# Rotary embedding of attention heads: gathering the rotated rows of all heads before turning them

## The chip, the cores and the metric

The kernel runs on one core of one Trainium2 chip. The metric is the device time of one execution in microseconds (us), and a kernel's time is the median of its runs. TensorE, the matrix engine, works beside VectorE, ScalarE and GpSimd; SyncE and ScalarE issue the transfers of this kernel. The engines run their own lists of instructions and wait for one another by semaphores. In the profile they are PE, DVE, ACT, POOL and SP.

## The reference

One layer over 512 tokens of width 1024, in fp32: a gated feed-forward network, a token mixer, and a second network, each followed by a layer norm of the input and the result. The mixer has two branches, sliding-window attention with sinks and a gated recurrence (HGRN2). Here only the attention's rotation matters: of each head's 64 values the first 16 are turned by an angle that depends on the token, in 16 heads of queries and 4 of keys.

```python
def partial_rope(t, cos, sin):
    half = ROPE_DIM // 2            # ROPE_DIM = 16, HEAD_DIM = 64
    t1, t2, rest = tf[..., :half], tf[..., half:ROPE_DIM], tf[..., ROPE_DIM:]
    return concatenate([t1 * cos - t2 * sin, t2 * cos + t1 * sin, rest], axis=-1)

q_a = partial_rope(q_a.reshape(B, S, N_Q_HEADS, HEAD_DIM), cos, sin)
k_a = partial_rope(k_a.reshape(B, S, N_KV_HEADS, HEAD_DIM), cos, sin)
y_attn = sliding_window_attention(q_a, k_a, v_a, sinks)
```

In the attention a block of 128 tokens sees its own block and the one before, and `exp(sink - m)` is added to the denominator of the softmax.

## The kernel before

**The products.** A matmul in fp32 is made of three in a rounded type: an operand is cut into a high part (`split`, a cast on ScalarE, L85) and a low part (the difference on VectorE, L86), called `whi` and `wlo` for weights. Each matrix of 1024 x 512 weights (a quad) goes through the class `Quads` in seven products of 24 matmuls of 128x256 each (`mul`, L276 to L293), in the order f1, then the previous quad's m4 and m3, f5, f6, f2, f7. Copies of sums in PSUM are kept by ScalarE (L313: `m1` after f1, `vs` after f6, `u3` after f7); VectorE adds them to others (L378, L323, L329) and makes the sums of weights (L308). A pipeline of depth 1 has the operands of the next product split while the present one runs. The pools are rings: four places for `whi` and `wlo`, five for raw weights, four PSUM banks named A for the products and four named B for all else.

**The side work.** Everything that is not such a product is put in between by the class `Side`: a list of generators, of which every half product takes as many steps as `side.rate` says; a step that yields `PAUSE` ends the turn. The rotation and the attention are such generators. The program runs `q_quad(0)`, then `gate_quad(0)` with `k_parts()` at its side (rate 1.0), then `gate_quad(1)`, `gate_quad(2)`, `q_quad(1)`, `gate_quad(3)` and a quad of the recurrence with `attention()` at their side (rate 3.0), L1021 to L1036. So the place of an instruction on its engine follows from these rates, and what the tile framework then makes of the order.

**The attention.** A tile holds two heads of 64 rows by 512 tokens. `k_parts` (L830) rotates the two key tiles and splits them for both partition halves. `q_quad(pp)` makes the queries of eight heads, four tiles; `q_parts(pp, ip)` (L857) adds the bias to each of two tiles (L865, ScalarE), rotates it and splits it into a high part (L871, ScalarE) and a low part (L872, VectorE). `chunk(pp, ip)` then goes over four blocks of tokens: `scores` (L889 and L890 on TensorE, the masking L894 on VectorE), `probs` (L901: exponentials on ScalarE by `func`, the sinks added in L912, sums and quotients in L916 to L920 on VectorE, transposes L124 on TensorE, copies L927 on ScalarE), and `weigh` (L942 on TensorE, copies L948 on ScalarE). `both` (L968) has the next `q_parts` run in between. For each of four chunks `q_parts` gives two tiles.

**The rotation.** `rope(dst)`, L797 to L802, works on a whole tile of 128 rows, though only 16 of each 64 are turned: the tables hold cos 1 and sin 0 for the other rows. It is four operations of VectorE on 128x512: a shuffle of rows within groups of 32 into `room(0)` (L799), times sin (L800), the tile times cos in place (L801), and the sum (L802). With two key tiles and eight query tiles that is ten sets.

Of the kernel before, what the change touches and what calls it, by code (L numbers as in the profile page):

```python
# [14 lines left out]
AF = mybir.ActivationFunctionType  # L15
ALU = mybir.AluOpType
# [6 lines left out]
S = 512  # L23
# [4 lines left out]
HD = 64  # L28
# [14 lines left out]
def body(ctx, tc, a):  # L43
    nc = tc.nc
# [31 lines left out]
    def big(i, shape=(P, 2, S), dtype=F32):  # L76

        return mid.tile(list(shape), dtype, name=f"g{i}")
# [42 lines left out]
    def transposed(blocks):  # L121
        tp = bank("B")
        for j, b in enumerate(blocks):
            nc.tensor.transpose(out=tp[:, j * P:(j + 1) * P], in_=b, identity=ident)  # L124
        return tp
# [74 lines left out]
    def func(**kw):  # L200


        with tc.issue_after(chain[-1]) if chain else ExitStack():
            chain.append(nc.scalar.activation(**kw).ins)
# [5 lines left out]
    PAUSE = object()  # L210
# [36 lines left out]
    side = Side()  # L247
# [19 lines left out]
    class Outs:  # L267
# [3 lines left out]
        def room(self, i):  # L271
            return self.rooms[i]
# [409 lines left out]
    def mix_const(name, shape, src=None, place=None):  # L682

        t = mc.tile(shape, F32, name=(place or name) + "_c")
        nc.sync.dma_start(out=t, in_=a[name] if src is None else src)
        return t
# [26 lines left out]
    cos_t = mix_const("rope_c", [P, S])  # L713
    sin_t = mix_const("rope_s", [P, S])
    amask = mix_const("amask", [P, 256])
    sink = mix_const("sinks", [P, NH], a["sinks"].broadcast_to([P, NH]))
# [22 lines left out]
    def bias(n, i):  # L739
        j = BCOL[n] + i  # L740
        return bcol[:, j:j + 1]
# [26 lines left out]
    def quad_to(src, d1, d2, done=None, mix=None):  # L768

        def finish(v):  # L770
            nc.scalar.copy(out=d2[:, :, :256], in_=v)
            if done:
                done()
        quads.quad(src, Outs((*thalves(d1), d2[:, :, 256:]), finish), mix)
# [17 lines left out]
    pairs = {0: Pair(0)}  # L792


    swap = [8 + i for i in range(8)] + list(range(8)) + list(range(16, 32))

    def rope(dst):  # L797
        rot = room(0)
        nc.vector.stream_shuffle(out=rot, in_=dst, mask=swap)  # L799
        nc.vector.tensor_tensor(out=rot, in0=rot, in1=sin_t, op=ALU.mult)  # L800
        nc.vector.tensor_tensor(out=dst, in0=dst, in1=cos_t, op=ALU.mult)  # L801
        nc.vector.tensor_tensor(out=dst, in0=dst, in1=rot, op=ALU.add)  # L802


    v_sb = big(5, [P, TT, 256])
# [18 lines left out]
    k_raw = [room(6 + j) for j in range(2)]  # L824
# [5 lines left out]
    def k_parts():  # L830


        k_hi.extend(big(i, dtype=F32R) for i in (4, 10))
        k_lo.extend(big(i, dtype=F32R) for i in (2, 11))
        for t in k_lo:
            nc.gpsimd.memset(t[top, 1].bitcast(F32), 0.0)
            nc.gpsimd.memset(t[bot, 0].bitcast(F32), 0.0)
        for j in range(2):
            t = k_raw[j]
            rope(t)  # L840
            yield
            for h, own in enumerate((top, bot)):
                for half in (top, bot):
                    nc.scalar.copy(out=k_hi[j][half, h], in_=t[own])
                nc.vector.tensor_tensor(out=k_lo[j][own, h], in0=t[own], in1=k_hi[j][own, h], op=ALU.subtract)
                yield

    q_raw = {}

    def q_quad(pp, mix=None):  # L850
# [3 lines left out]
            q_raw[pp] = d  # L854
        quad_to(a["w_q"][pp], d[0], d[1], done, mix)

    def q_parts(pp, ip):  # L857


        while pp not in q_raw:  # L860
            yield
        out = []
        for i in range(2):
            t = q_raw[pp][ip][:, i]
            nc.scalar.activation(out=t, in_=t, func=AF.Identity, bias=bias("q", 4 * pp + 2 * ip + i),  # L865
                                 scale=1.0 if ip == 0 else -1.0)
            rope(t)
            yield
            q = big(6 + 2 * ip + i, dtype=F32R)
            for h, (own, other) in enumerate(((top, bot), (bot, top))):  # L870
                nc.scalar.copy(out=q[own, h], in_=t[own])  # L871
                nc.vector.tensor_tensor(out=q[other, h], in0=t[own], in1=q[own, h], op=ALU.subtract)  # L872
                yield
            out.append(q)
        return out
# [25 lines left out]
    def probs(pp, n, ip, neg, nm):  # L901


        kb = 1 if n == 0 else 2
        sm = mxp.tile([P, 4], F32, name="sm", bufs=3)
        rd = mxp.tile([P, 4], F32, name="rd", bufs=3)
        for j in range(4):
            func(out=neg[j // 2][:, j % 2, :kb * P], in_=neg[j // 2][:, j % 2, :kb * P], func=AF.Exp,
                                 bias=nm[:, j:j + 1], scale=-1.0, accum_out=sm[:, j:j + 1])
        for hf in range(2):  # L910
            hh = 8 * pp + 4 * hf + 2 * ip
            nc.vector.tensor_tensor(out=rd[:, 2 * hf:2 * hf + 2], in0=nm[:, 2 * hf:2 * hf + 2],  # L912
                                    in1=sink[:, hh:hh + 2], op=ALU.add)
        yield
        func(out=rd, in_=rd, func=AF.Exp)
        nc.vector.tensor_tensor(out=rd, in0=rd, in1=sm, op=ALU.add)  # L916
        nc.vector.reciprocal(out=rd, in_=rd)
        for j in range(4):
            p_ = neg[j // 2][:, j % 2, :kb * P]
            nc.vector.tensor_scalar(out=p_, in0=p_, scalar1=rd[:, j:j + 1], scalar2=None, op0=ALU.mult)  # L920
        for _ in range(2):
            yield PAUSE
        tps = [transposed([neg[j // 2][:, j % 2, kk * P:(kk + 1) * P] for j in range(4)]) for kk in range(kb)]
        pts = []
        for kk in range(kb):
            pt = neg[kk].rearrange("p i c -> p (i c)") if n % 2 else room(6 + kk)
            nc.scalar.copy(out=pt, in_=tps[kk])  # L927
            pts.append(pt)
        return pts
# [21 lines left out]
    def chunk(pp, ip, qs):  # L951
        h = 4 * pp + 2 * ip
        pts = []
        ahead = yield from scores(pp, 0, ip, qs)
        for n in range(TT):
            now = ahead
            if n + 1 < TT:
                ahead = yield from scores(pp, n + 1, ip, qs)
            pts.append((yield from probs(pp, n, ip, *now)))
            yield PAUSE  # L960
            if n % 2:
                y = room(5, [P, 2, 2, P])
                weigh(pp, n - 1, pts[-2:], y)
                nc.sync.dma_start(out=ya_dram[h:h + 2, :, (n - 1) * P:(n + 1) * P].rearrange("i p c -> p i c"),
                                  in_=y.rearrange("p i n c -> p i (n c)"))
                yield
# [16 lines left out]
    def attention():  # L983
        qs = yield from q_parts(0, 0)
        for i in range(4):
            for _ in range(2):
                yield PAUSE
            if i < 3:
                nxt = yield from both(chunk(i // 2, i % 2, qs), q_parts((i + 1) // 2, (i + 1) % 2), 3)
                side.marks.append(i)  # L990
                qs = nxt
            else:
                yield from chunk(1, 1, qs)
# [24 lines left out]
    def gate_quad(i):  # L1018
        quads.quad(a["w_" + ("ga", "gh")[i // 2]][i % 2], Gates(i))

    q_quad(0, mix)  # L1021
    side.add(k_parts())
    side.rate = 1.0
    gate_quad(0)
    pipe.pump()
    side.add(attention())
    side.rate = 3.0
    gate_quad(1)
    gate_quad(2)
    while len(side.marks) < 1:  # L1030
# [287 lines left out]
def _rope_rows():  # L1318
    half = HD // 8
    inv = np.float32(500000.0) ** (-np.arange(0, 2 * half, 2, dtype=np.float32) / np.float32(2 * half))  # L1320
    ang = np.arange(S, dtype=np.float32)[:, None] * inv[None, :].astype(np.float32)
    cos, sin = np.cos(ang).T, np.sin(ang).T
    c = np.ones((HD, S), np.float32)
    s = np.zeros((HD, S), np.float32)
    c[:half], c[half:2 * half] = cos, cos
    s[:half], s[half:2 * half] = -sin, sin
    return np.concatenate([c, c]), np.concatenate([s, s])


# [59 lines left out]
```

## Time and profile before

| | |
|---|---|
| median of 3 runs | 1254.51 us (1254.0 to 1255.38) |
| profiled execution | 1255.64 us, its span 1253.8 us |
| granted clock of TensorE, mean | 0.997 |
| TensorE busy | 1228.7 us, 98% |
| VectorE busy | 992.0 us, 79% |
| ScalarE busy | 646.7 us, 52% |
| GpSimd busy | 37.1 us, 3% |

The span is what the profiler saw between the first and the last instruction; a run's time has some 2 us around it. The chain of work that ended last is followed back from the last instruction, at each step to what released it. A matmul's end is modelled, since matmuls are pipelined, so the distance between starts is the better measure of TensorE's pace. An idle time is shown with what ended it. In the windows, PEclk is the granted clock of TensorE as a share of its full 2.4 GHz.

### The profile page before, as it was taken

Reading aid. Unit: us, or ns where it says so; the run is one execution under the profiler, and the core shown is the slowest. Engines: PE = TensorE matmul, PEld = TensorE weight load, DVE = VectorE, ACT = ScalarE, POOL = GpSimd, SP = SyncE. Lnnn points to the kernel's source line nnn. Section 1 sums busy time; section 2 is a strip of 40 time slices with the busy share of each in tenths; the row PEclk is TensorE's granted clock in tenths of the full one; section 3 lists DMA queues with packets and bytes.
Section 4 is the critical chain, followed back from the end, with each engine's and each line's share of the span. In section 5 each row is a group of like instructions: output and inputs, shape, how many; then the busy total and the mean of one; then the engine's idle time right before and its main releaser. Section 6 shows DMA issues by size and latency. Waiting matters only on the chain.

```text
span 1253.8 us, 21589 instructions
## 1 busy us (share of the span) xinstructions
PE 1228.7 (98%) x8918; PEld 1155.2 (92%) x8918; DVE 992.0 (79%) x1389; ACT 646.7 (52%) x916; POOL 37.1 (3%) x37
## 2 busy tenths in 40 slices
PE   9999999999999999999999999999999999999997
PEld 9999999888899989989999998788899999998886
DVE  7988878983499999898878787564899887789535
ACT  5554455642247667677654765442364445466210
POOL 0000000000000000000001011000100000000001
PEclk9999999999999999999999999999999999999999
DMA  7433332742232344233223243653333333345301
GB/s 264 140 98 116 102 101 85 234 131 89 101 139 83 111 133 138 86 109 104 87 70 117 86 158 111 238 193 132 118 116 121 102 102 102 116 128 193 118 34 68
DMA packets 51715, 152.84 MB, mean 122 GB/s; under 512 B 5792, under 2 KB 12960, under 8 KB 51616
## 3 DMA queue, kind: packets, MB, share of 16 engines
q1 hardware_dynamic: 47296, 137.29, 32.9%
q10 hardware_dynamic: 4320, 14.16, 3.4%
q8 instruction: 70, 1.15, 0.4%
q14 instruction: 29, 0.24, 0.1%
HBM read 136.75 MB, written 14.68 MB: 121 GB/s over the span
## 4 chain that ended last, share of the span: by engine, by line
PE 80%; DVE 13%; DMA 2%; issue 2%; POOL 1%; ACT 1%; SPq 0%; DVEq 0%; ACTq 0%; POOLq 0%
PE A L293 47%; PE A L119 5%; PE A L118 5%; PE A L117 5%; PE A L618 4%; DVE wlo L86 3%; PE B L118 3%; PE B L117 3%; PE B L119 3%; DVE x L86 2%; PE B L124 2%; PE B L942 1%; POOL rstd L447 1%; DVE g L452 1%; PE B L618 1%
## 5 line engine op out<-in xcount | busy, mean ns | idle before, releaser
L293 PE MATMUL A<-x,whi 128*128 128x256 f32 x3840 | 544.1, 284 | 4.2 <-ACT u L313 3.1
L293 PEld LDWEIGHTS A<-x,whi 128*128 128x128 f32 x3840 | 496.1, 192 | 6.8 <-ACT u L313 4.1
L85 ACT CAST whi<-raw 128x1024 fp32r<-128x1024 f32 (+1 forms) x182 | 188.5, 1041 | 260.2 <-PE A L119 102.7
L293 PE MATMUL A<-x,wlo 128*128 128x256 f32 x1920 | 311.6, 284 | 0.2 <-DVE wlo L86 0.2
L86 DVE TENSOR_TENSOR wlo<-raw,whi 128x1024 fp32r<-128x1024 f32 (+1 forms) x182 | 219.3, 1208 | 114.1 <-ACT whi L85 113.7
L293 PEld LDWEIGHTS A<-x,wlo 128*128 128x128 f32 x1920 | 265.7, 192 | 0.9 <-issue 0.4
L85 ACT CAST whi<-wsum 128x1024 fp32r<-128x1024 f32 x140 | 146.5, 1049 | 154.1 <-PE A L293 118.3
L86 DVE TENSOR_TENSOR wlo<-wsum,whi 128x1024 fp32r<-128x1024 f32 x140 | 170.2, 1219 | 7.1 <-ACT whi L85 6.9
L117 PE MATMUL A<-whi,x 128*128 128x256 f32 (+1 forms) x280 | 87.7, 313 | 0.0
L118 PE MATMUL A<-wlo,x 128*128 128x256 f32 (+1 forms) x280 | 87.5, 313 | 0.0
L119 PE MATMUL A<-whi,x 128*128 128x256 f32 (+1 forms) x280 | 86.9, 311 | 0.0
L308 DVE TENSOR_TENSOR wsum<-raw 128x1024 f32<-128x1024 f32 x64 | 77.5, 1219 | 9.7 <-DMA raw<-in_w_dram 8.4
L308 DVE TENSOR_TENSOR wsum<-raw,wsum 128x1024 f32<-128x1024 f32 x64 | 78.1, 1220 | 0.6
L117 PE MATMUL A<-x,whi 128*128 128x512 f32 (+1 forms) x160 | 59.9, 374 | 0.1
L119 PE MATMUL A<-x,wlo 128*128 128x512 f32 (+1 forms) x160 | 59.3, 371 | 0.5 <-DVE wlo L86 0.5
L118 PE MATMUL A<-x,whi 128*128 128x512 f32 (+1 forms) x160 | 59.0, 369 | 0.0
L117 PEld LDWEIGHTS A<-whi,x 128*128 128x128 f32 x280 | 53.3, 190 | 3.0
L119 PEld LDWEIGHTS A<-whi,x 128*128 128x128 f32 x280 | 53.2, 190 | 2.9
L118 PEld LDWEIGHTS A<-wlo,x 128*128 128x128 f32 x280 | 53.3, 191 | 2.6
L86 DVE TENSOR_TENSOR x<-g,x 128x512 fp32r<-128x512 f32 (+1 forms) x57 | 47.9, 861 | 6.2 <-ACT x L85 6.1
L618 PE MATMUL A<-whi,x 128*128 128x512 f32 x192 | 51.1, 389 | 0.0
L85 ACT CAST x<-g 128x512 fp32r<-128x512 f32 (+1 forms) x57 | 42.2, 765 | 16.2 <-DVE g L1262 4.6
(202 smaller groups left out, 1632.6 us busy)
## 6 DMA issues: line engine op xcount, KB each, us to landing
raw<-in_w_dram SPq DMA_DIRECT2D x134, 512.0 KB, 3.4
raw<-in_w_fqg_dram SPq DMA_DIRECT2D x24, 512.0 KB, 3.7
raw<-in_w_q_dram SPq DMA_DIRECT2D x8, 512.0 KB, 3.8
raw<-in_w_ga_dram SPq DMA_DIRECT2D x8, 512.0 KB, 3.3
raw<-in_w_gh_dram SPq DMA_DIRECT2D x8, 512.0 KB, 4.7
raw<-in_w_i_dram SPq DMA_DIRECT2D x8, 512.0 KB, 3.6
raw<-in_w_pa_dram SPq DMA_DIRECT2D x8, 512.0 KB, 4.3
g<-x_spill ACTq DMA_DIRECT2D x8, 512.0 KB, 5.0
```

Source lines behind the costliest of these rows:

```text
L85: nc.scalar.copy(out=hi, in_=src)
L86: nc.vector.tensor_tensor(out=lo, in0=src, in1=hi, op=ALU.subtract)
L117: nc.tensor.matmul(out, lhsT=lh, rhs=rh, start=first, stop=False, **kw)
L118: nc.tensor.matmul(out, lhsT=lh, rhs=rl, start=False, stop=False, **kw)
L119: nc.tensor.matmul(out, lhsT=ll, rhs=rh, start=False, stop=last, **kw)
L124: nc.tensor.transpose(out=tp[:, j * P:(j + 1) * P], in_=b, identity=ident)
L293: nc.tensor.matmul(reg, lhsT=w, rhs=x, start=first, stop=last, skip_group_check=True)
L308: nc.vector.tensor_tensor(out=t, in0=x, in1=y, op=ALU.add)
L447: nc.gpsimd.tensor_tensor(out=rstd, in0=ve, in1=pw, op=ALU.pow)
L452: nc.vector.scalar_tensor_tensor(out=r[:, c], in0=r[:, c], scalar=rstd, in1=b_bc[:, c], op0=ALU.mult, op1=ALU.add)
L618: nc.tensor.matmul(bk[j], lhsT=op[n][:, x, 2 * h + k, js], rhs=w[:, k * 512:(k + 1) * 512], start=first, stop=last, skip_group_check=True)
L942: mm = nc.tensor.matmul(o[hf][hf * HD:(hf + 1) * HD, i * 256:(i + 1) * 256], lhsT=v_sb[:, n + i + 1 - kb + kk, g * HD:(g + 1) * HD], rhs=p ...
```

## The change

`rope` takes a list of tiles. It gathers the 16 turned rows of each head into one tile by transfers that ScalarE issues (L805), each 16x512, 32 KB: four for the two key tiles, eight for the four query tiles of one `pp`. It then shuffles them (L808) into a PSUM bank of name B, multiplies by the tables (L809, L811), adds (L812), and sends the rows back by as many transfers (L816), with `PAUSE` steps in between. The tables hold the 16 rows of cos and sin eight times. A new generator `q_turned(pp)` adds the bias to all four query tiles (L877) and rotates them together; for `pp` 0 it stands in the side list behind `k_parts`, for `pp` 1 at the start of `q_parts(1, 0)`. The two additions of sinks per block become one of four columns (L932). The rates become 2.0 and 3.5.

```diff
-    def rope(dst):
-        rot = room(0)
-        nc.vector.stream_shuffle(out=rot, in_=dst, mask=swap)
-        nc.vector.tensor_tensor(out=rot, in0=rot, in1=sin_t, op=ALU.mult)
-        nc.vector.tensor_tensor(out=dst, in0=dst, in1=cos_t, op=ALU.mult)
-        nc.vector.tensor_tensor(out=dst, in0=dst, in1=rot, op=ALU.add)
+    def rope(tiles):
+        rows = [t[i * HD:i * HD + 16] for t in tiles for i in range(2)]
+        both, rot = room(0)[:16 * len(rows)], bank("B")[:16 * len(rows)]
+        parts = [both[16 * i:16 * i + 16] for i in range(len(rows))]
+        n = both.shape[0]
+        for x, y in zip(rows, parts):
+            nc.scalar.dma_start(out=y, in_=x)
+        for _ in range(2):
+            yield PAUSE
+        nc.vector.stream_shuffle(out=rot, in_=both, mask=swap)
+        nc.vector.tensor_tensor(out=rot, in0=rot, in1=sin_t[:n], op=ALU.mult)
+        yield
+        nc.vector.tensor_tensor(out=both, in0=both, in1=cos_t[:n], op=ALU.mult)
+        nc.vector.tensor_tensor(out=both, in0=both, in1=rot, op=ALU.add)
+        for _ in range(2):
+            yield PAUSE
+        for x, y in zip(rows, parts):
+            nc.scalar.dma_start(out=x, in_=y)
+        for _ in range(2):
+            yield PAUSE
...
+        yield from rope(k_raw)
         for j in range(2):
             t = k_raw[j]
-            rope(t)
-            yield
...
+    def q_turned(pp):
         while pp not in q_raw:
             yield
+        tiles = [q_raw[pp][ip][:, i] for ip in range(2) for i in range(2)]
+        for i, t in enumerate(tiles):
+            nc.scalar.activation(out=t, in_=t, func=AF.Identity, bias=bias("q", 4 * pp + i),
+                                 scale=1.0 if i < 2 else -1.0)
+            yield
+        yield from rope(tiles)
+
+    def q_parts(pp, ip):
+        if (pp, ip) == (1, 0):
+            yield from q_turned(1)
         out = []
         for i in range(2):
             t = q_raw[pp][ip][:, i]
-            nc.scalar.activation(out=t, in_=t, func=AF.Identity, bias=bias("q", 4 * pp + 2 * ip + i),
-                                 scale=1.0 if ip == 0 else -1.0)
-            rope(t)
-            yield
...
-        for hf in range(2):
-            hh = 8 * pp + 4 * hf + 2 * ip
-            nc.vector.tensor_tensor(out=rd[:, 2 * hf:2 * hf + 2], in0=nm[:, 2 * hf:2 * hf + 2],
-                                    in1=sink[:, hh:hh + 2], op=ALU.add)
+        four = sink.rearrange("p (a h b i) -> p a h b i", a=2, h=2, b=2)[:, pp, :, ip]
+        nc.vector.tensor_tensor(out=rd.rearrange("p (h i) -> p h i", h=2), in0=nm.rearrange("p (h i) -> p h i", h=2),
+                                in1=four, op=ALU.add)
...
     side.add(k_parts())
-    side.rate = 1.0
+    side.add(q_turned(0))
+    side.rate = 2.0
     gate_quad(0)
     pipe.pump()
     side.add(attention())
-    side.rate = 3.0
+    side.rate = 3.5
```

Three places show how the order of instructions moves. The first is ScalarE at the end of `gate_quad(0)`. Names carry the buffer's number; `g0` and `g1` hold queries, `whi` of a `raw` is here the operand of the next quad's first product, and `A_4184` (`A_4185` after) is the bank of the last product. Before:

```order
L85 CAST whi_4350<-wsum_4135 128x1024
L85 CAST whi_4420<-raw_4408 128x1024
L865 ACTIVATE g0_3971<-g0_3971,b_col_c_3703 128x512
L85 CAST whi_4424<-raw_4129 128x1024
L313 COPY vs_4345<-A_4184 128x512
L865 ACTIVATE g0_3971<-g0_3971,b_col_c_3703 128x512
L85 CAST whi_4466<-wsum_4319 128x1024
L85 CAST whi_4507<-wsum_4416 128x1024
L313 COPY u3_4406<-A_4184 128x512
L313 COPY m1_4459<-A_4428 128x512
L871 CAST g6_4461<-g0_3971 64x512 x2
```

After:

```order
L313 COPY vs_4352<-A_4185 128x512
L877 ACTIVATE g1_3972<-g1_3972,b_col_c_3703 128x512
L805 DMA r0_4416<-g0_3971 16x512 x4
L805 DMA r0_4416<-g1_3972 16x512 x2
L313 COPY u3_4414<-A_4185 128x512
L805 DMA r0_4416<-g1_3972 16x512 x2
L85 CAST whi_4438<-raw_4426 128x1024
L85 CAST whi_4442<-raw_4129 128x1024
L85 CAST whi_4477<-wsum_4323 128x1024
L85 CAST whi_4515<-wsum_4434 128x1024
L313 COPY m1_4471<-A_4446 128x512
L816 DMA g0_3971<-r0_4416 16x512 x4
```

The cast for the next quad's first product (`whi_4420` before, `whi_4438` after) stood ahead of the copies `vs` and `u3`; it now stands behind both, with two issues of row copies in between. The returns stand behind four casts and `m1`.

The second is VectorE over the same products, from the difference of that cast (`wlo_4421` before, `wlo_4439` after). Before:

```order
L86 TENSOR_TENSOR wlo_4421<-raw_4408,whi_4420 128x1024
L378 TENSOR_TENSOR g3_4379<-m1_4209,A_4354 128x512
L86 TENSOR_TENSOR wlo_4425<-raw_4129,whi_4424 128x1024
L799 STREAM_SHUFFLE r0_4442<-g0_3971 128x512
L86 TENSOR_TENSOR wlo_4467<-wsum_4319,whi_4466 128x1024
L800 TENSOR_TENSOR r0_4442<-r0_4442,rope_s_c_3707 128x512
L801 TENSOR_TENSOR g0_3971<-g0_3971,rope_c_c_3705 128x512
L323 TENSOR_TENSOR g3_4379<-u3_4406,A_4287 128x512
L802 TENSOR_TENSOR g0_3971<-g0_3971,r0_4442 128x512
L86 TENSOR_TENSOR wlo_4508<-wsum_4416,whi_4507 128x1024
L872 TENSOR_TENSOR g6_4461<-g0_3971,g6_4461 64x512 x2
```

After:

```order
L86 TENSOR_TENSOR wlo_4439<-raw_4426,whi_4438 128x1024
L86 TENSOR_TENSOR wlo_4443<-raw_4129,whi_4442 128x1024
L808 STREAM_SHUFFLE B_4417<-r0_4416 128x512
L86 TENSOR_TENSOR wlo_4478<-wsum_4323,whi_4477 128x1024
L809 TENSOR_TENSOR B_4417<-B_4417,rope_s_c_3707 128x512
L811 TENSOR_TENSOR r0_4416<-r0_4416,rope_c_c_3705 128x512
L86 TENSOR_TENSOR wlo_4516<-wsum_4434,whi_4515 128x1024
L812 TENSOR_TENSOR r0_4416<-r0_4416,B_4417 128x512
L308 TENSOR_TENSOR wsum_4559<-raw_4430,wsum_4436 128x1024
L308 TENSOR_TENSOR wsum_4594<-raw_4432,wsum_4559 128x1024
L329 TENSOR_TENSOR r8_4543<-vs_4352,A_4288 128x512
L893 TENSOR_TENSOR g6_4549<-g0_3971,g6_4549 64x512 x2
```

Before, one tile's rotation and its differences stood ahead of the next tile's rotation; after, one set serves all four tiles, and the first differences follow it.

The third is VectorE at the first scores of the second half (`pp` 1), after the change; `B_5859` to `B_5898` are the scores' banks.

```order
L308 TENSOR_TENSOR wsum_6049<-raw_5779,wsum_5980 128x1024
L893 TENSOR_TENSOR g6_5815<-g0_5139,g6_5815 64x512 x2
L893 TENSOR_TENSOR g7_5820<-g0_5139,g7_5820 64x512 x2
L893 TENSOR_TENSOR g8_5873<-g1_5140,g8_5873 64x512
L915 ISA r1_5856,nm_5858<-B_5859,amask_c_3709,nsink_3713 128x128
...
L915 ISA r4_5895,nm_5896<-B_5898,amask_c_3709,nsink_3713 128x256
...
L932 TENSOR_TENSOR rd_5912<-nm_5858,sinks_c_3711 128x4
L893 TENSOR_TENSOR g8_5873<-g1_5140,g8_5873 64x512
L936 TENSOR_TENSOR rd_5912<-rd_5912,sm_5911 128x4
L329 TENSOR_TENSOR r8_5967<-vs_5725,A_5658 128x512
L937 RECIPROCAL rd_5912<-rd_5912 128x4
L86 TENSOR_TENSOR wlo_5983<-wsum_5980,whi_5982 128x1024
```

Before, two differences and the first maskings of `pp` 1 stood apart, with products' operands in between:

```order
L86 TENSOR_TENSOR wlo_5869<-raw_5469,whi_5868 128x1024
L872 TENSOR_TENSOR g6_5658<-g0_5089,g6_5658 64x512 x2
L799 STREAM_SHUFFLE r0_5695<-g0_5089 128x512
L378 TENSOR_TENSOR g3_5766<-m1_5565,A_5741 128x512
L800 TENSOR_TENSOR r0_5695<-r0_5695,rope_s_c_3707 128x512
L801 TENSOR_TENSOR g0_5089<-g0_5089,rope_c_c_3705 128x512
L86 TENSOR_TENSOR wlo_5910<-wsum_5707,whi_5909 128x1024
L802 TENSOR_TENSOR g0_5089<-g0_5089,r0_5695 128x512
L308 TENSOR_TENSOR wsum_6025<-raw_5815,wsum_5821 128x1024
L872 TENSOR_TENSOR g7_5700<-g0_5089,g7_5700 64x512 x2
```

After the change five differences, eight maskings and a sixth difference stand in a row, with no operand of a product among them.

## Rows read from the trace of the kernel before

**Rows 1.** The page: the chain that ended last, by engine.

```profile
PE 80%; DVE 13%; DMA 2%; issue 2%; POOL 1%; ACT 1%; SPq 0%; DVEq 0%; ACTq 0%; POOLq 0%
```

**Rows 2.** The chain in order of time: start us, us, engine, tile, line.

```profile
377.69 44.64 PE A L293 x372
...
438.56 0.40 DVE r L894
...
441.00 1.06 ACT whi L85
...
442.10 4.88 PE A L293 x37
```

**Rows 3.** Windows: us, busy PE, PEld, DVE, ACT, POOL, PEclk, DMA share, GB/s.

```profile
422.00:463.00 41.00, 37.93 (x293) 35.61 (x291) 39.65 (x98) 30.95 (x68) 0.00 (x0) 0.96 0.30 99
...
509.00:557.00 48.00, 45.73 (x366) 43.02 (x367) 47.46 (x114) 34.02 (x73) 0.00 (x0) 1.00 0.26 88
...
509.00:533.00 24.00, 23.01 (x185) 22.21 (x184) 23.66 (x53) 16.50 (x34) 0.00 (x0) 1.00 0.27 91
```

**Rows 4.** VectorE by line and form, 377 to 595 us: busy us, mean ns.

```profile
L799 DVE STREAM_SHUFFLE r<-g 128x512 f32<-128x512 f32 x8 | 5.9, 738 | 0.1
...
L912 DVE TENSOR_TENSOR rd<-nm,sinks_c 128x2 f32<-128x2 f32 x32 | 3.6, 152 | 0.0
```

**Rows 5.** Timeline of VectorE, 412 to 427 us: start us, us, engine, line.

```profile
412.55 1.21 DVE L86 TENSOR_TENSOR wlo<-wsum,whi 128x1024 fp32r<-128x1024 f32 x1
413.68 0.69 DVE L800 TENSOR_TENSOR r<-r,rope_s_c 128x512 f32<-128x512 f32 x1
414.28 0.69 DVE L801 TENSOR_TENSOR g<-g,rope_c_c 128x512 f32<-128x512 f32 x1
...
417.33 1.40 DVE L872 TENSOR_TENSOR g<-g,g 64x512 fp32r<-64x512 f32 x2
...
426.27 0.34 DVE L894 CUSTOM_DVE_ANT_0 r<-B,amask_c,nsink 128x128 f32<-128x128 f32 x1
...
426.53 0.35 DVE L894 CUSTOM_DVE_ANT_0 r<-B,amask_c,nsink 128x128 f32<-128x128 f32 x1
```

**Rows 6.** Timeline of ScalarE's queue at two issues: start us, us.

```profile
854.66 0.34 ACTq L462 DMA_DIRECT2D g_bc<-in_ln_g_dram  x1
855.04 0.90 ACTq L463 DMA_DIRECT2D b_bc<-in_ln_b_dram  x1
```

**Rows 7.** Timeline of TensorE, 414 to 449 us; brackets: idle before, releaser.

```profile
414.96 1.12 PE L293 MATMUL A<-x,whi 128*128 128x256 f32 x8
...
424.94 0.33 PE L889 MATMUL B<-g,g 128*128 128x128 f32 x1 [1.22 <-DVE g L872]
...
428.40 1.53 PE L293 MATMUL A<-x,whi 128*128 128x256 f32 x8
...
440.61 1.22 PE L293 MATMUL A<-x,whi 128*128 128x256 f32 x8 [0.68 <-ACT u L313]
...
448.97 1.52 PE L942 MATMUL B<-r,g 128*64 128x256 f32 x12 [0.70 <-ACT r L927]
```

**Rows 8.** Timeline of ScalarE, 415 to 424 us.

```profile
415.17 0.59 ACT L313 COPY m<-A 128x512 f32<-128x512 f32 x1 [1.78 <-PE A L293]
...
423.55 1.25 ACT L871 CAST g<-g 64x512 fp32r<-64x512 f32 x2
```

**Rows 9.** DMA issues: count, KB each, median us from issue to landing.

```profile
raw<-in_w_gh_dram SPq DMA_DIRECT2D x8, 512.0 KB, 4.7
...
yh_dram<-r SPq DMA_DIRECT2D x8, 256.0 KB, 2.0
```

**Rows 10.** Windows around the first scores, columns as in rows 3.

```profile
422.00:426.00 4.00, 2.67 (x21) 2.27 (x19) 3.89 (x7) 3.95 (x6) 0.00 (x0) 0.99 0.19 66
426.00:429.30 3.30, 3.30 (x17) 3.30 (x17) 3.30 (x14) 3.27 (x10) 0.00 (x0) 0.50 0.23 79
```

More of the change, by code (lines that the diff above doesn't have):

```diff
@@ L792, in body @@
     pairs = {0: Pair(0)}
-    swap = [8 + i for i in range(8)] + list(range(8)) + list(range(16, 32))
-    def rope(dst):
-        rot = room(0)
-        nc.vector.stream_shuffle(out=rot, in_=dst, mask=swap)
-        nc.vector.tensor_tensor(out=rot, in0=rot, in1=sin_t, op=ALU.mult)
-        nc.vector.tensor_tensor(out=dst, in0=dst, in1=cos_t, op=ALU.mult)
-        nc.vector.tensor_tensor(out=dst, in0=dst, in1=rot, op=ALU.add)
+    swap = [16 * i + (j + 8) % 16 for i in range(2) for j in range(16)]
+    def rope(tiles):
[18 more added lines that the diff above has]
+            yield PAUSE
     v_sb = big(5, [P, TT, 256])
@@ L855, in q_quad @@
         quad_to(a["w_q"][pp], d[0], d[1], done, mix)
-    def q_parts(pp, ip):
+    def q_turned(pp):
         while pp not in q_raw:
             yield
+        tiles = [q_raw[pp][ip][:, i] for ip in range(2) for i in range(2)]
[7 more added lines that the diff above has]
+            yield from q_turned(1)
         out = []
@@ L1322, in _rope_rows @@
     cos, sin = np.cos(ang).T, np.sin(ang).T
[L1323 to L1327, printed above, removed]
+    return np.tile(np.concatenate([cos, cos]), (8, 1)), np.tile(np.concatenate([-sin, sin]), (8, 1))
 def kernel(**inputs):
```

## The prediction

> **What bounds the kernel now.** I read the chain's shares by engine first: 80% is TensorE's work and 13% VectorE's [rows 1]. So a change to VectorE can pay only where VectorE is that 13%. The table by stage says where: the rotations lie between 378 and 557 us, and there I counted the matmuls of each stretch. Where TensorE is never held up, 372 of its 128x256 matmuls take 44.64 us, 0.12 us each [rows 2]. From 422 to 463 us it did 293 in 41 us, so 41 - 293 x 0.12 = 5.8 us were lost; from 509 to 557 it did 366 in 48 us, 4.1 us lost, of it 24 - 185 x 0.12 = 1.8 us by 533 [rows 3]. These are upper bounds, since a trace can lack a matmul. VectorE is busy for 39.65 of 41 and 47.46 of 48 us there, ScalarE for 31 and 34. So some 10 us in 1254 are all that cheaper rotations could give, if nothing is added.
>
> **What VectorE saves.** A rotation is a shuffle and three operations of 128x512. The shuffle has 0.74 us; the others follow one another 0.60 us apart (413.68, 414.28), so a set costs 0.65 to 0.74 + 3 x 0.60, about 2.5 us [rows 4, 5]. Ten sets become three: 7 x 2.5 = 17.5 us less. Of the sinks, 32 additions at 0.152 us become 16 [rows 4]: 16 x 0.15 = 2.4 us of busy time at most, about 1 us if the wider one starts as late. The shuffle's result and one source of two operations move to PSUM; no row here shows a shuffle into it, so I leave the price and allow a tenth of a us for each either way, 0.3 in all for a set.
>
> Not all of it falls where TensorE waits. The two key sets lie before 422 us, where TensorE runs at full pace already [rows 2]: one set less there is worth nothing, its cover being VectorE's lead over TensorE's products. If that cover went, it would be 2.5 us.
>
> **What the row copies add.** Forty transfers of 32 KB are issued by ScalarE: 8 for the keys, 16 for each half of the queries. Two issues on ScalarE's queue begin 0.38 us apart [rows 6]. Eight in a row hold the queue for 3.0 us, forty for 15.2 us. ScalarE has idle time, so the total decides nothing; what decides is who stands behind them. The eight key issues stand well ahead of need, and I cost them at nothing, covered by the same lead.
>
> **First place: the end of the first gate quad.** Before, the cast for the next quad's first product is made early, ahead of the quad's last two copies. In the changed order it stands behind the copy of the last product, `u3`, and two issues. TensorE ends that product at 412.08 us (24 matmuls before 414.96) and can't go on until that cast is made [rows 7]. The step: a copy starts 0.21 us after its product (at 415.17, where the next product begins at 414.96) and takes 0.59; a cast takes 1.06 and its matmul starts 0.04 later (442.10 after 441.00 + 1.06); of the two issues (0.76) I take half, an estimate between an issue that runs beside its neighbour and one that doesn't [rows 2, 6, 7, 8]. That is 0.21 + 0.59 + 0.38 + 1.06 + 0.04 = 2.3 us of standstill where there was none. Bounds: 1.9 with free issues; 4.5 if an issue must also wait for an earlier load to land (several carry a wait for an earlier transfer): a load of 512 KB has a median of 4.7 us from issue to landing, a store of 256 KB 2.0 [rows 9].
>
> **The first scores.** TensorE then has four products to do: 412.08 + 2.3 + 4 x 2.88 = 425.9 us. VectorE, from the cast on (414.2), has four differences at 1.13, the shuffle and three operations: 414.2 + 4.5 + 0.65 + 1.8 = 421.2 us [rows 5]. Behind the last of these stand the eight returns on ScalarE: 421.2 + 3.0 = 424.3. Then come one copy (0.58) and four casts of 64x512, two of which take 1.25 us [rows 8]: 424.3 + 0.6 + 2.5 = 427.4. The last difference, 0.7 us (two take 1.40) [rows 5], ends at 428.2, and the eight scores of the first block end at about 429.1. The other eight take 0.96 us. So at 430.0 us four products and sixteen scores are done; the trace of before has the same work done at 428.40 [rows 7]. The change is 1.7 us behind here, though before lost 2.9 us on the way: it waited 1.22 us for the second of its rotated tiles, and then ran at half clock, 0.50 with 17 matmuls in 3.3 us, the 1.2 GHz level [rows 7, 10]. I take one such spell as before; a second one, after the new standstill, would add 3.3 - 17 x 0.12 = 1.3 us.
>
> Here a rule stands against my price. The Trainium skill, page "DMA: Bandwidth & Descriptors", section "Issuing engines are not separate DMA queues", says that the sequencer's time to start a transfer is usually small beside the transfer. The rows don't bear this out for small copies: eight issues, 3.0 us, against 2.0 us to landing [rows 6, 9]. With issues at nothing the sum below would be 1.5 us less (third rival).
>
> **The rest of the first half.** Of the 5.8 us, 2.9 are left behind 428.4. In them two query sets, 5 us of VectorE's work, go. But the idle time that the rows name there is ScalarE's: 0.68 us for the copy `u3` and 0.70 for a copy of probabilities [rows 7]. That leaves about 1.5 us which VectorE can answer for; I take 0.6 back, between 0 and 2.9.
>
> **The second half.** VectorE does four sets fewer and one more, 7.5 us less. But the order packs the first scores of the second key pair: five differences of 0.7, eight maskings (four at 0.27, four at 0.40 us), then a sixth difference, 0.6 + 3 x 0.12 for small ones and the 1.13 that TensorE's product waits for: 3.5 + 2.7 + 0.7 + 1.0 + 1.1 = 9.0 us [rows 2, 5]. Within that time TensorE has a first wait of 0.7 and 16 scores and 25 matmuls, 41 x 0.12 = 4.9: 5.6 us. So 3.4 are lost, less 0.3 for differences that overlap by their tails (two take 1.40, not all of it their own), 3.1. Before lost 1.8 in that place. That is 1.3 more. The other 2.3 us lost to 557 I leave. Bounds: all 4.1 vanish, or as much again is lost.
>
> **Sum.** +1.7 - 0.6 + 1.3 = +2.4 us. Against the profiled execution, 1255.64 us (span 1253.8), this is 1258.0; that execution stands 1.1 us over the median of the runs, 1254.51, so I forecast **1256.9 us**. A measurement of this kernel can tell about 0.2%, 2.5 us: this is no change that can be told, on the slow side. Its own range is 1253.5 to 1259.5: at one end all 2.9 us of the first half come back and 1.1 of the second's, at the other there is a second half-clock spell and 1.3 us more in the second half.
>
> **Rivals.**
> *VectorE was the bound, and the packing is harmless (faster).* For it: busy 97% and 99% in the two stretches, and the chain there runs through VectorE's maskings [rows 2, 3]. Then the 2.9 behind 428.4 and the 4.1 us vanish, and only the 1.7 stays: 1254.5 - 7.0 + 1.7 = 1249.2. Against it: the two idle times of ScalarE's, and casts and copies that now stand behind issues. 0.25.
> *ScalarE's queue is held by the copies (slower).* An issue that waits for a 512 KB load stops every cast behind it. Its place is the end of the first gate quad: 4.5 us in place of 2.3, and the clock at half once more, 1.3: 1256.9 + 3.5 = 1260.4. It decides from a standstill of about 4 us on. Against it: the transfers' engines are busy for 0.30 and 0.26 of these stretches [rows 3], so a load seldom stands long. 0.15.
> *Issuing costs nothing.* The sequencer runs ahead, and only landing counts: at the first scores 421.2 + 2.0 = 423.2 in place of 424.3, 1.1 less [rows 9], and 0.4 less at the end of the quad: 1256.9 - 1.5 = 1255.4. The rule of the Trainium skill is this case. 0.16.
>
> **Chances.** Forecast 0.44, of it 0.23 within 0.2% and 0.21 slower; faster rival 0.25; held queue 0.15, slower; free issues 0.16, of it 0.14 same and 0.02 faster. So faster 0.27, same 0.37, slower 0.36. The range that holds eight in ten is 1249.0 to 1261.0: it takes in the faster rival's value and the held queue's, and leaves out their further ends.
>
> **What would show it.** In the profile after: 12 rotating operations in the attention and 40 issues on ScalarE about 0.38 us apart; TensorE idle for some 2.3 us near 412 us with the cast as releaser; a wait of about 3 us for the differences ahead of the first scores; VectorE's busy time down by about 20 us. It is wrong if TensorE has no gap near 412, if the first sixteen scores and four products are done by 428, or if the second half's first scores lose under 2 us.

## The result and the profile after

The changed kernel takes 1261.61 us (median of 4 runs, 1261.24 to 1262.26) where the kernel before, run beside it, took 1254.95 (1254.0 to 1255.4): ratio 1.0055, interval 1.0037 to 1.0072. It is 6.7 us slower. Forecast were 1256.9 us and a range up to 1261.0. The profiled execution has a span of 1260.2 us against 1253.8.

VectorE was relieved, by a little less than forecast. The page of the changed kernel, busy time by engine:

```profile
PE 1231.5 (98%) x8918; PEld 1157.9 (92%) x8918; DVE 974.8 (77%) x1338; ACT 646.1 (51%) x916; POOL 37.2 (3%) x37
```

VectorE is busy for 17.2 us less than the 992.0 of before. One operation of a set costs what it did or a little less (the shuffle 689 ns against 738), by line and form (busy us, mean ns), against [rows 4]:

```profile
L808 DVE STREAM_SHUFFLE B<-r 128x512 f32<-128x512 f32 x2 | 1.4, 689 | 0.0
...
L932 DVE TENSOR_TENSOR rd<-nm,sinks_c 128x4 f32<-128x4 f32 x16 | 2.5, 156 | 0.0
```

So the time went elsewhere. Both kernels issue the same products in the same order, so I compared when the same matmul starts in the two traces, lined up on a matmul at 127 us. A positive lag is the changed kernel behind. Where one kernel has done scores that the other has yet to do, as at 533 and 550 us, the lag holds their time as well:

| product starts, before (us) | lag of after (us) | what lies between |
|---|---|---|
| 409 | -0.1 | keys, their rotation |
| 412 | 2.4 | end of the first gate quad |
| 418 | 4.0 | half clock |
| 432 | 6.4 | first scores, half clock again |
| 443 | 4.9 | some comes back |
| 515 | 5.1 | rest of the first half |
| 533 | 1.5 | queries of the second half; its first 16 scores before, none after |
| 550 | 7.4 | first scores of the second half |
| 598 | 6.3 | the attention's end; constant from here on |

TensorE's timeline after, at the three places (idle before it, and what ended that):

```profile
414.42 1.58 PE L293 MATMUL A<-x,whi 128*128 128x256 f32 x11 [2.39 <-ACT whi L85]
...
429.95 0.48 PE L910 MATMUL B<-g,g 128*128 128x128 f32 x1 [2.27 <-DVE g L893]
...
543.78 1.19 PE L293 MATMUL A<-x,whi 128*128 128x256 f32 x8 [3.02 <-DVE rd L937]
```

And ScalarE with its queue (ACTq) over the first two and ahead of the third:

```profile
412.06 0.58 ACT L313 COPY u<-A 128x512 f32<-128x512 f32 x1 [3.94 <-DMA r<-g]
412.12 1.16 ACTq L805 DMA_DIRECT2D r<-g  x2
413.32 2.00 ACT L85 CAST whi<-raw 128x1024 fp32r<-128x1024 f32 x2 [0.67 <-ACT u L313]
...
421.46 5.00 ACTq L816 DMA_DIRECT2D g<-r  x8
428.08 0.58 ACT L1035 COPY r<-A 128x512 f32<-128x512 f32 x1 [8.10 <-DMA g<-r]
428.56 2.54 ACT L892 CAST g<-g 64x512 fp32r<-64x512 f32 x4
...
526.97 6.44 ACTq L816 DMA_DIRECT2D g<-r  x8
533.45 2.55 ACT L892 CAST g<-g 64x512 fp32r<-64x512 f32 x4 [6.51 <-DMA raw<-in_w_fqg_dram]
```

Eight returns hold the queue for 5.0 us and 6.44 us, where I had 3.0. ScalarE's casts of the query rows start at 428.56 behind them and one copy, and only then can VectorE make the differences that the scores wait for. Of the 6.44 us not all is issuing. The seventh return is issued by 531.39, the eighth begins at 532.89, and the release named at the cast is a load of weights, 512 KB, that SyncE issued at 528.10 (duration ns, and from issue to landing):

```profile
L90 SPq DMA_DIRECT2D raw<-in_w_fqg_dram x1: 328/328/328, 528.1 to 528.1; - x1
...
DMA to landing us min/median/max: 4.8/4.8/4.8
```

It landed at 532.87, on the semaphore on which the eighth return then reports. So this issue waited 1.5 us for a load, and the casts with it. The wait ahead of the copy L1035 (8.10 us, put down to the returns) also has another end: a store of 256 KB out of the copy's buffer landed at 428.00, 0.08 us before the copy began. The windows, answering to [rows 3] and [rows 10], show the lost time with VectorE no longer full, and two spells of the lower clock (0.50 and 0.51, the 1.2 GHz level):

```profile
422.00:463.00 41.00, 38.55 (x291) 36.64 (x290) 34.76 (x81) 29.62 (x66) 0.00 (x0) 0.92 0.30 97
509.00:557.00 48.00, 44.79 (x363) 42.72 (x362) 37.98 (x83) 31.60 (x64) 0.00 (x0) 1.00 0.29 90
...
416.60:419.20 2.60, 2.60 (x14) 2.60 (x14) 2.60 (x6) 0.61 (x1) 0.00 (x0) 0.50 0.96 251
...
432.00:436.50 4.50, 4.50 (x22) 4.38 (x22) 3.91 (x12) 4.46 (x6) 0.00 (x0) 0.51 0.18 42
```

From 422 to 463 us VectorE's busy time fell from 39.65 to 34.76 us, and TensorE did 291 matmuls in place of 293. What an issue costs is seen at the two lines of copies (duration ns min/median/max):

```profile
L816 ACTq DMA_DIRECT2D g<-r x16: 514/548/602, 421.5 to 532.9; - x16
...
L805 ACTq DMA_DIRECT2D r<-g x16: 514/600/1372, 406.4 to 519.4; - x16
```

### The profile page after: what moved, and what is told of

Read it like the earlier page. It is cut to its first block, busy times and chain, and to the rows that moved or that the text cites. A ratio compares the mean times of both kernels' runs of the same rounds, so it can differ in the third digit from the quotient of the medians.

```text
span 1260.2 us, 21615 instructions
## 1 busy us (share of the span) xinstructions
PE 1231.5 (98%) x8918; PEld 1157.9 (92%) x8918; DVE 974.8 (77%) x1338; ACT 646.1 (51%) x916; POOL 37.2 (3%) x37
## 4 chain that ended last, share of the span: by engine, by line
PE 43%; DVE 6%; DMA 1%; POOL 1%; issue 1%; ACT 1%; DVEq 0%; SPq 0%; POOLq 0%; ACTq 0%
PE A L293 22%; PE A L119 4%; PE A L118 4%; PE A L117 4%; PE A L618 2%; PE B L117 2%; PE B L118 2%; PE B L119 2%; DVE wlo L86 1%; PE B L1138 1%; DVE x L86 1%; PE B L124 1%; POOL rstd L447 1%; DVE g L452 1%; POOL rs L1180 0%
```

## The experiments

All medians stand beside the kernel before on the same chip; lags are read as in the table above, at 515 us (the first half's end) and at 598 us.

### Orders or issues: the first three runs

Theory 1 was that three orders of instructions cost the time (the cast behind `u3`; the casts of query rows behind the copy L1035, which by the order waits for a store; the packed differences). Theory 2 was that ScalarE's issuing costs it.

```diff
     gate_quad(0)
-    pipe.pump()
     side.add(attention())
```

> The changed kernel without the emptying of the pipeline between the first gate quad and the attention, so that the cast for the next quad's first product stands ahead of the copy u3 and the row copies again; nothing else is edited. Theory 1 (three places, each an order of instructions): the stop of 2.4 us at 412 us and the half-clock spell behind it are gone, the kernel is 4.1 us earlier at 423 us, and most of it stays: 1257.5 to 1258.5 us. Theory 2 (the time that ScalarE spends on issuing the 40 copies is what costs, wherever the cast stands): the first scores wait for the returns as long as before, and at most 1.5 us are won: 1260 us or more.

Measured: 1262.94 us, ratio 1.0055 (1.0043 to 1.0067). Nothing was won. The cast now was made at 407.57, but the three last gathers stood ahead of the next cast. ScalarE and its queue in this run, then TensorE:

```profile
412.23 3.13 ACTq L805 DMA_DIRECT2D r<-g  x3
415.40 1.04 ACT L85 CAST whi<-raw 128x1024 fp32r<-128x1024 f32 x1 [2.60 <-DMA r<-g]
```

```profile
416.50 1.21 PE L293 MATMUL A<-x,whi 128*128 128x256 f32 x8 [1.44 <-ACT whi L85]
429.37 0.33 PE L910 MATMUL B<-g,g 128*128 128x128 f32 x1 [3.68 <-DVE g L893]
```

The stop of 2.39 us became one of 1.44 a product later, and the wait for the first scores grew from 2.27 to 3.68. The run is 1.9 us behind at 418 us in place of 4.0, but 6.2 at 432 in place of 6.4. So theory 1 fell at this place: whichever cast stands first, another one stands behind the issues. Three issues take 3.13 us here because the last of them, too, waited for a load: the second had ended at 413.38, and the third began at 414.85, 0.03 us after 512 KB that SyncE had issued at 409.90 had landed.

```diff
-                self.now = room(8, [P, 2, 256])
+                self.now = room(7 if i == 3 and self.dst is gate_dram['ga'] and self.at == 0 else 8, [P, 2, 256])
```

> The changed kernel with the first gate quad's last copy (L1035) put into another buffer, so that it doesn't wait for the store of the buffer's earlier content; it then stands ahead of the returns in ScalarE's order. Theory 1: the four casts of the query rows start when the returns are issued, at about 426.5 in place of 428.6 us, and the first scores come some 2 us earlier; total 1259.5 to 1260.5 us. Theory 2: the casts wait for the returns to be issued and landed anyway; within 0.5 us of the changed kernel, 1261.6.

Measured: 1261.64 us, ratio 1.0045 (1.0031 to 1.0058). The casts began right behind the eighth return, at 428.94 in a trace that runs 2.42 us later, that is at 426.52, as theory 1 had it. Between 418 and 432 us the lag grew by 1.2 us in place of 2.4, so that wait is worth some 1.2 us there. At 515 us the run is 2.7 behind in place of 5.1, but the second half then loses 2.8 in place of 1.2, and at 598 us it is 5.5 behind against 6.3. Total: no difference that can be told, which is theory 2's range.

> Both edits of the two runs before. Theory 1: 4.1 and 2 us are won, less 1 to 1.5 that came back later anyway: 1256.0 to 1257.5 us, about 1 to 3 us over the kernel before. Theory 2: no more than 2 us won, 1259.5 us or more.

Measured: 1260.05 us, ratio 1.0035 (1.0022 to 1.0047). At most 2 us were won, as theory 2 had it: 1.8 by 515 us (3.3 behind), of which the second half lost 2.0 again.

### Another queue for the copies

```diff
-            nc.scalar.dma_start(out=y, in_=x)
+            nc.gpsimd.dma_start(out=y, in_=x)
...
-            nc.scalar.dma_start(out=x, in_=y)
+            nc.gpsimd.dma_start(out=x, in_=y)
```

> The changed kernel with all 40 row copies issued by GpSimd, which has next to nothing else to do; nothing else is edited, but the cast of the first place then stands early by itself. Theory 1: the first two places go (6 us, less 1.5 that came back), the third, where VectorE's differences and maskings stand packed, stays at some 3 us: 1256 to 1258 us. Theory 2: with ScalarE free of issues all three go and VectorE's relief shows: 1253 us or less.

Measured: **1250.3 us**, ratio 0.9958 (0.9944 to 0.9972): 11.3 us less than the changed kernel (each beside its own runs of the kernel before) and 5.1 less than before. The second theory was nearer, and the third place went as well. Up to 515 us only two idle times of TensorE are left in this run, neither for a cast; behind it there are two more, of 0.18 and 0.28 us:

```profile
434.37 0.33 PE L124 MATMUL B<-ident,r 128*128 128x128 f32 x1 [1.46 <-DVE r L940]
469.85 0.53 PE L124 MATMUL B<-ident,r 128*128 128x128 f32 x2 [0.57 <-DVE r L940]
```

And VectorE's relief reaches TensorE: the windows of this run.

```profile
422.00:463.00 41.00, 39.43 (x324) 36.67 (x322) 36.72 (x89) 31.86 (x71) 0.00 (x0) 1.00 0.47 147
509.00:557.00 48.00, 47.29 (x383) 44.00 (x381) 44.36 (x103) 35.07 (x76) 4.22 (x9) 1.00 0.36 113
```

324 and 383 matmuls stand against 293 and 366 of before [rows 3]. This run changes two things, the queue and what the framework then does with the order (the early cast came by itself), so it does not tell them apart alone.

### Which half, and is it the issue itself?

The next two runs give `rope` the queue as an argument: GpSimd for the keys and `pp` 0 in the first, for `pp` 1 in the second, ScalarE for the rest.

```diff
-        yield from rope(tiles)
+        yield from rope(tiles, nc.gpsimd if pp == 0 else nc.scalar)
```

> The changed kernel with the copies for the keys and for the first half of the queries issued by GpSimd, those for the second half by ScalarE as before. Theory 3 (what costs is ScalarE's queue: an issue holds it for 0.5 to 0.65 us, longer where an earlier transfer has not landed, and casts and copies wait behind): the first half goes like that of the run with all copies on GpSimd, 3.2 us ahead of the kernel before at 510 us, and the second half loses 1.2 us as in the changed kernel: 2 us faster than before, 1252.5 to 1254.0 us. Theory 4 (the second half's place at 540 us sets its own time, whenever the first half ends): most of the first half's gain is lost there, 1257 us or more.

> The reverse: copies for the second half of the queries issued by GpSimd, the others by ScalarE. Theory 3: 5.1 us behind the kernel before at 510 us as the changed kernel, then 1.6 us won as in the run with all on GpSimd: 1258 to 1259.5 us. Theory 4: the second half takes up the whole lag, 1255 us or less.

Measured: 1254.4 us, ratio 0.999 (0.998 to 1.0), and 1256.74 us, ratio 1.0017 (1.0006 to 1.0027). By the times, 1254.4 is 0.4 over theory 3's range and 1256.74 is 1.3 under it; theory 4 had 1257 or more and 1255 or less, and both miss. The lags add up as theory 3 has it, by sign and roughly by size:

| copies issued by ScalarE in | lag at 515 us | change from 515 to 598 us |
|---|---|---|
| both halves (the change) | 5.1 | +1.2 |
| both, cast early | 4.7 | +3.6 |
| both, copy L1035 in another buffer | 2.7 | +2.8 |
| both, the two edits together | 3.3 | +3.2 |
| first half only | 3.4 | -1.9 |
| second half only | -3.2 | +2.0 |
| neither (GpSimd) | -3.2 | -1.6 |
| neither (SyncE) | -1.9 | -1.4 |

Issuing by ScalarE costs the first half 5.9 to 8.3 us (2.7 to 5.1 against -3.2) and the second 2.8 to 5.2 (1.2 to 3.6 against -1.6). In five of these runs ScalarE issues the second half's copies in the same way, and the changed kernel's 1.2 is the least of the five; why they differ is open. From 598 to 1000 us the lag of some runs still moves by up to 1.2 us, so small differences here tell nothing.

```diff
             nc.gpsimd.dma_start(out=y, in_=x)
+            if len(tiles) > 2:
+                nc.scalar.dma_start(out=rows_dram[rows_n[0] % 64], in_=x)
+                rows_n[0] += 1
```

The same was added at the returns. Nobody reads these rows.

> All copies that count issued by GpSimd, and beside each of the 32 for the queries one more of the same rows issued by ScalarE into a room in device memory that nobody reads. Theory 3 (the issue itself on ScalarE's queue): most of the 11 us come back, 1257 us or more. Theory 5 (waiting for the rows to land, not the issue, is what costs): nobody waits for these, within 1.5 us of the run without them, 1250.3.

Measured: 1259.64 us, ratio 1.0033 (1.0022 to 1.0044). 32 more issues on ScalarE gave back 9.3 of the 11.3 us. GpSimd's returns do wait for those added transfers that read the rows which they overwrite, but these had landed by 413.86 and 518.15 us, before the returns began at 416.40 and 522.01. At the first query set the queue held a cast for TensorE's next product, and in the second half a copy (ScalarE, then TensorE's two longest stops):

```profile
419.57 4.60 ACTq L824 DMA_DIRECT2D rows_dram<-r  x5
424.22 1.05 ACT L85 CAST whi<-wsum 128x1024 fp32r<-128x1024 f32 x1 [4.12 <-DMA rows_dram<-r]
```

```profile
413.87 2.05 PE L293 MATMUL A<-x,whi 128*128 128x256 f32 x15 [1.62 <-ACT whi L85]
...
529.55 2.08 PE L293 MATMUL A<-x,whi 128*128 128x256 f32 x8 [2.75 <-ACT u L313]
```

So theory 5 fell: between 400 and 600 us TensorE stops mostly for casts and copies of ScalarE's (5.4 us) and for differences of its casts (2.5), and nowhere for scores whose rows had not landed, although GpSimd's returns took up to 6.2 us to land here against 3.5 without the added transfers. It is what stands behind an issue on ScalarE. The late cast is back as well (the stop of 1.62 us), so this run, too, holds the order that comes with issuing from ScalarE.

The trace tells what the hold is made of. In the 4.60 us the five issues take 2.76 by themselves. Another 1.5 us pass until a load of 512 KB, which SyncE issued at 417.27, has landed at 423.32; the fourth issue begins at 423.39. In the second half the eighth issue waits 3.6 us in the same way, for a load that landed at 528.49. So both count: an issue's own time, and a wait for an earlier transfer that it carries. How the 9.3 us divide between the two is not shown.

> All 40 copies issued by SyncE, whose queue also issues the weights' loads. Theory 3: ScalarE is free of them, so as with GpSimd unless a row copy that waits for VectorE holds a load behind it that is needed: 1250 to 1253 us. If the loads behind the waiting copies come late, 1255 us or more.

Measured: 1251.2 us, ratio 0.997 (0.996 to 0.9981). SyncE does nearly as well; between 400 and 600 us TensorE never waited for a load there.

### The small parts, and the best version

> The run with all copies issued by GpSimd, with the rates of the side work as before the change, 1.0 and 3.0. If the gain is VectorE's relief alone, the rates matter little: 1249.5 to 1252 us. If the faster side work is what made it fast (the gathering needs PAUSE steps, so slow rates put the first scores later and pack the rest), 1254 us or more.

Measured: 1252.94 us, ratio 0.9986 (0.9977 to 0.9995); the lag at 598 us is -4.5, against -4.9 with the new rates. By the runs' times the old rates lose some of the gain; the time lies between the two that were expected.

> The kernel before with the new rates 2.0 and 3.5 and nothing else. If the rates are a part of the gain with GpSimd by themselves, 1253 us or less; if they only push more of VectorE's work into the stretches that it already bounds, no change or slower, 1254 to 1257 us.

Measured: 1256.69 us, ratio 1.0016 (1.0006 to 1.0027): the rates alone are no gain.

> The kernel before with the two additions of the sinks made one of 128x4 and nothing else. 16 operations of 0.15 us less on VectorE: 2.4 us at most, some 1 us where it is what TensorE waits for; within 1.2 us of the kernel before, 1253.5 to 1255.5 us. If it shifts the order in the packed places, up to 2 us either way.

Measured: 1253.67 us, ratio 0.9993 (0.9984 to 1.0002), no difference that can be told.

> The run with all copies on GpSimd, with the two edits of the third run beside it (the pipeline not emptied, the first gate quad's last copy in another buffer). With ScalarE's queue free the cast is early and no copy holds the casts, so there is little left to win: 1249.5 to 1251 us, no difference from 1250.3 that can be told. If the copy L1035 still held the query casts, 1 to 2 us less.

Measured: 1249.47 us, ratio 0.9961 (0.9948 to 0.9973). With all copies on GpSimd, the cast early and the other buffer, the kernel is 5 us faster than before; from the run with GpSimd alone (0.9958) it can't be told apart.

## Why the prediction was wrong

**What VectorE saves: nearly right.** 17.2 us less busy time; forecast were 17.5 for the sets and 1 to 2.4 for the sinks, "about 20" among the signs. The key sets were worth nothing and their copies cost nothing: the lag is -0.1 at 409 us.

**First place: right in time.** 2.39 us of standstill, with the cast as releaser, forecast 2.3. The two issues held the cast for 0.67 us behind the copy, where I had 0.38; a shorter delay ahead of the copy made up for it. But a half-clock spell came behind it, 0.50 with 14 matmuls in 2.6 us. I had named it as a second spell that would add 1.3 and left it out of the sum; it added 1.6 (2.4 to 4.0).

**First scores: the step that failed.** "The change is 1.7 us behind here" became 6.4. VectorE's set ended at 421.4 as worked out (421.2). But I had priced an issue at 0.38 us, the distance between two loads of 512 KB, and had passed over the 0.90 us of the second of them [rows 6]. A copy of rows between two tiles holds ScalarE's queue for 0.51 to 0.65 us, the median 0.60, so the eight returns took 5.0 us and ended at 426.46 in place of 424.3. The copy behind them I had priced without its wait, 1.6 us for a store, and it began at 428.08. The casts so began at 428.56, 3.7 us later than my 424.9, and the next product at 432.22; and the clock then fell a second time, to 0.51. I had taken one spell for the whole; there were two. So two terms of the sum were mis-sized, the eight issues (3.0, measured 5.0) and the number of spells, and one was put at nothing without a reason, the copy's wait (1.6). Two of the sums in that paragraph are 0.1 off (414.3 and 424.2), which changes nothing.

**The rest of the first half: right in size.** 0.6 us forecast to come back, 1.3 came (6.4 to 5.1). I had put it down to VectorE's share; but before, TensorE stood idle here for ScalarE alone (0.68 and 0.70 us in [rows 7], and 0.28 for a cast), and after the change none of that is left, only 0.15 and 0.53 us for VectorE. Why ScalarE came earlier there was not tried.

**The second half: right in its sum, in part by luck.** Forecast 1.3 lost, measured 1.2; the stop worked out as 3.1 us measured 3.02. The eight returns ahead of the casts, 6.44 us, stood in no term of it. Not foreseen was that 3.6 us come back before it, from 515 to 533, and that the place then loses more than the stop, 5.9 us from 533 to 550. Much of that is only put off: the 16 scores that lie between 515 and 533 us before, 1.9 us at 0.12 each, come in the later stretch. The packed differences wait for the casts, and those for the returns. The five differences in a row, on VectorE:

```profile
534.86 3.56 DVE L893 TENSOR_TENSOR g<-g,g 64x512 fp32r<-64x512 f32 x5
...
543.64 1.19 DVE L86 TENSOR_TENSOR wlo<-wsum,whi 128x1024 fp32r<-128x1024 f32 x1
```

That is 8.8 us from the first difference to the start of the operand that TensorE waits for and 9.9 to the next start behind it, where I had 9.0. In four other runs with the same issues the half lost 2.0 to 3.6.

**The sum.** 6.4 - 1.3 + 1.2 = 6.3 us of lag stand against 1.7 - 0.6 + 1.3 = 2.4. The first scores, with the spell ahead of them, miss by 4.7 us; the other two terms take 0.8 of it back.

**The rivals.** ScalarE's queue held by the copies came true in kind and, by luck, in time (1260.4 for 1261.6), with a chance of 0.15. Its place was wrong: the 3.5 us were worked out for a wait for a load at the end of the gate quad, and the loss came from eight issues in a row ahead of the scores, twice. What it named, an issue that waits for a load of 512 KB and stops the casts behind it, did happen, 1.5 us long in the second half, and in the run with the early cast at the very place that it had named. "VectorE was the bound" (1249.2) comes near a kernel whose ScalarE does not issue, 1250.3, though that kernel does not lose the 1.7 us which the rival kept. The error was to say that "the total decides nothing" and to price only what stands behind the copies at two places. The third rival, free issues, fell: 32 issues whose rows nobody reads cost 9.3 us. The Trainium skill, page "DMA: Bandwidth & Descriptors", section "Issuing engines are not separate DMA queues", calls the sequencer's time usually small beside the transfer. The trace does not agree for these copies: an issue has medians of 0.55 and 0.60 us and its copy 2.0 to landing, and eight in a row hold the queue for 5.0.

## What to carry to other kernels

A transfer issued from a computing engine's list takes time in that list, here 0.51 to 0.65 us each: count this and the wait for an earlier transfer that it may carry (1.5 us here), not the transfer's own time, and list what stands behind it, all the more where many stand in a row ahead of the work that the bound engine waits for. Try small copies on an engine that has little else to do; the same change then was a gain of 5 us instead of a loss of 7. Price an issue from one of the same kind, or widen the range by the difference.

## What was not expected of the hardware

In these runs an issue's time went with what it moved. 16x512 rows from tile to tile took ScalarE 0.51 to 0.65 us, apart from a single one of 1.37; the same rows to device memory took 0.31 us at the least and 0.38 or 0.43 in the median, with two of 1.39 and 1.56. GpSimd took 0.484 us for each of the former (ns min/median/max of this line in the run with GpSimd):

```profile
L805 POOL DMA_DIRECT2D r<-g x16: 484/484/487, 404.3 to 508.9; - x16
```

What held the queue longer were waits. In five runs the eighth return of the second half began 0.02 to 0.03 us after a load of SyncE's on the same semaphore had landed, 1.1 to 2.0 us after the seventh had ended. GpSimd's eight returns of the first half, without such a wait, take 3.81 us.

And the same standstill of 2.39 us at the same product was followed by a clock of 0.50 in the changed kernel, yet by 1.00 in the run with the other buffer (416.60 to 423 us) and in that with ScalarE issuing in the first half only. ScalarE's order is the same in the three up to that cast, so what a standstill costs by the clock, 1.6 us here, may come or not.
